# Tile 0's expert dots: from the sweep over all experts to gathered rows

## The chip, the core and the metric

The kernel runs on one core of a Trainium2 chip. The metric is the device time of one launch in microseconds; three runs of the kernel before gave a median of 3764.14 us (3752.35 to 3771.85).

## The reference

One step of a one-layer hybrid decoder: a prompt of 1024 tokens and eight sequences of four sample tokens. Each layer projects the normed input, runs dilated attention and an RWKV-7 scan, projects out, and then applies PEER, a layer of 16,384 single-neuron experts of which each token uses 128 (8 heads of 16). All of the change is in PEER:

```python
def one(hb):                                   # hb: tokens x 1024
    q = (hb @ w_pq).reshape(chunk, PEER_HEADS, 2, PEER_HALF)
    s = jnp.einsum('nhpc,hpkc->nhpk', q, sub_keys).astype(jnp.float32)
    ...                                        # top 16 of 256 sums per head: eid, gate
    act = jax.nn.gelu(jnp.einsum('nd,nhkd->nhk', hb, expert_u[eid]), approximate=False)
    return jnp.einsum('nhk,nhkd->nd', gate * act, expert_v[eid])
```

For one token this is the sum over its 128 experts of gate x gelu(u . h) x v, with u and v rows of 1024 numbers of the tables `expert_u` and `expert_v`.

## The kernel before

The prompt's 1024 tokens are eight tiles of 128; the 32 sample tokens are a ninth, `NT`. PEER is computed in two ways.

- **By gathered rows** (tiles 5, 6, 7 and `NT`, 416 units in all). A unit is one of the 128 picks of each token of a tile. `gathered` lets POOL issue an indirect DMA that fetches 128 rows of 4 KB (one per token) of `expert_u`; VectorE multiplies them by h2 and sums along the row in one instruction (tile `row`, result in a column of `co`). h2 stands in PSUM there (tile `gh`), and so does the running sum of the second half, in which the rows of `expert_v` are gathered, scaled by `co` and added (tiles `gh` and `ga`). Five `row` buffers are in use.
- **Densely** (tiles 0 to 4, 640 tokens). All 16,384 experts are evaluated for all tokens on TensorE, in 128 blocks of 128 experts, and a table of gates that is zero where an expert was not picked selects. `hidden(b)` multiplies the block's `expert_u` by h2T, each operand split into a high and a low part (`uh`, `ul`), so three matmuls for each of 8 pieces of the depth, in two halves of 320 tokens; then gelu on ScalarE, a product with the gates `g` and a split into `ch`, `cl` on ScalarE and VectorE. `output` multiplies these by the block's `expert_v` rows (`vh`, `vl`), in groups of four blocks, for 5 tiles x 2 halves of the columns, and VectorE adds the result to `dacc`. POOL makes `ul` and most of `vl`.

The table of gates, `g_d` in DRAM, is written in the front part by `spread_gates`: for each token TensorE multiplies two one-hot rows (`oha`, scaled by the gate, made by POOL and ScalarE; `ohb`, made by VectorE) into a 128 x 128 table (PSUM tag `sp`), ScalarE copies it to `stage`, and SP stores it.

The program has three parts that matter here. Up to about 700 us come norms, projections and the first scans. In the front part (to 1702 us) several generators are woven: `delta`, the last two RWKV scans, with high priority, and beside it as fill `front` (out-projection and h2 of a tile), `scores`, `picks` (which ends with `eid`, the experts' numbers), `spreads` and `attention`; after `delta` the sample's scan and attention take its place. In the dense part the 128 blocks are fill, and `gather_all` with the routing of tiles 6, 7 and `NT` is the main stream. A scheduler turns the woven program into one fixed order per engine, and each engine runs its order strictly in turn. The metered costs in `_Meter` decide how the generators are woven.

All instructions are issued through one helper, so the profile shows line 196 (197 in the changed kernel) for nearly all; operations are told apart by their tiles.

Of the kernel before, what the change touches and what calls it, by code (L numbers as in the profile page):

```python
# [11 lines left out]
FT = mybir.dt.float32  # L12
FR = mybir.dt.float32r
# [6 lines left out]
D = 1024  # L20
# [19 lines left out]
NROW = 5  # L40
NW = 3
# [160 lines left out]
def tile_hybrid_step(ctx, tc, ins, outs):  # L202
# [1077 lines left out]
    def project_out(pa, pp, tiles, new_x1, new_h2, bufs=NW):  # L1280
# [34 lines left out]
        for j, i in enumerate(tiles):  # L1315
# [28 lines left out]
            if i not in dense_set:  # L1344
# [72 lines left out]
    def route_pick(pick, tops, i, eng=ve):  # L1417
# [5 lines left out]
        fi = pa.tile([128, 16, TOPK], FT, tag="tf", name="tf", bufs=1)[:, :2 * nh]  # L1423
# [29 lines left out]
        pf = pa.tile([128, H, TOPK], I32, tag="te", name="te", bufs=1)[:, :nh]  # L1453
        ve.tensor_scalar(pf, pu.bitcast(I32), 14, None, op0=OP.logical_shift_left)
# [41 lines left out]
    dots = {}  # L1496

# [55 lines left out]
    def spread_gates(pa, pp, i, c0, iota128, stages):  # L1553

        eid, gts = eids[i][i], gates[i][i]
        keys = pa.tile([128, 2, 128], I32, tag="keys", name="keys", bufs=1)
# [58 lines left out]
    def dense(pa, pp, acc, h2T, tiles):  # L1615
# [7 lines left out]
        def hidden(b):  # L1623
# [9 lines left out]
            for h in range(2):  # L1633
                if b % 4 == 0:
                    G_[h] = pa.tile([128, n // 64, 4, 32], FT, tag="g", name="g", bufs=3)
                    sy.dma_start(G_[h], g_d[n // 64 * h:n // 64 * (h + 1), :, b:b + 4].rearrange("s e i t -> e s i t"))
                cs = slice(h * n // 2, (h + 1) * n // 2)
                ps = pp("d")
                for k in range(KD):
                    mm3(ps[:, :n // 2], (uh[:, k], ul[:, k]), [x[:, k, cs] for x in h2T], k == 0, k == KD - 1)  # L1640

                t = ps[:, :n // 2]
                sc.activation(t, t, AF.Gelu)
                tv = t.rearrange("p (s t) -> p s t", t=32)
                ve.tensor_tensor(tv, tv, G_[h][:, :, b % 4], op=OP.mult)
                split(t, ch[:, cs], cl[:, cs])
# [130 lines left out]
    dense_set = [0, 1, 2, 3, 4]  # L1777
# [9 lines left out]
    h2_f = dram.tile([128, KD, NDENSE], FT, name="h2_f")  # L1787
    hcol = {i: 128 * i for i in dense_set}
    with ExitStack() as es:
# [5 lines left out]
        open_picked(es, "picked_A", dense_set, 2)  # L1795
# [204 lines left out]
```

## Time and profile before

| | |
|---|---|
| median of 3 runs | 3764.14 us (3752.35 to 3771.85) |
| the profiled execution's own time | 3753.1 us |
| its span | 3751.3 us |
| mean granted TensorE clock | 0.967 |
| TensorE, VectorE, POOL, ScalarE busy | 92%, 72%, 55%, 38% |
| first dense matmul | 1704 us |

"Busy" of an engine is the time in which one of its instructions runs. Matmuls overlap each other, so their cost is read from start to start, not from their duration. A `DMA_INDIRECT` row of POOL is the issue alone; the data land later. What a stretch costs is read from the windows of that stretch, and what holds an engine up from what it waited for.

### The profile page before, as it was taken

What the parts mean: (1) busy time and instruction counts of PE and PEld (TensorE: products, weight loads), DVE (VectorE), ACT (ScalarE), POOL (GpSimd) and SP (SyncE); (2) the same over time, 40 slices, a digit from 0 to 9 for tenths busy, and PEclk for the clock granted to TensorE, in tenths of its full rate; (3) what the DMA queues carried; (4) which work ended last, traced back from release to release, by engine and by line L of the source; (5) the groups of instructions that cost most, each with busy time, mean ns of one, the idle gap of its engine ahead of it and who ended that gap; (6) DMA issues with size and microseconds to landing.
All of it is one profiled execution on the core that took longest, in us unless ns stands there. A gap on an engine that the chain in (4) does not pass through costs nothing.

```text
span 3751.3 us, 57270 instructions
## 1 busy us (share of the span) xinstructions
PE 3453.9 (92%) x19618; PEld 2873.9 (77%) x19618; DVE 2693.2 (72%) x6059; ACT 1431.2 (38%) x3122; POOL 2080.6 (55%) x1842
## 2 busy tenths in 40 slices
PE   7999999789888988988999989999999999999998
PEld 3878678567767755556777778988888888898997
DVE  2556365588688656785778998787777877777787
ACT  5645345336765754543221122322223222222321
POOL 2342011015545446754655677777777777776784
PEclk8999999899999989998999999999999999999999
DMA  9653596553675568749988779999999999999997
GB/s 293 197 148 117 176 285 186 151 182 130 225 233 166 189 229 255 244 149 309 320 316 298 262 255 334 340 321 322 327 323 324 329 320 322 315 330 318 336 336 256
DMA packets 592528, 981.58 MB, mean 262 GB/s; under 512 B 78323, under 2 KB 354620, under 8 KB 589420
## 3 DMA queue, kind: packets, MB, share of 16 engines
q1 hardware_dynamic: 467788, 524.84, 43.9%
q0 software_dynamic: 124448, 453.08, 34.1%
q8 instruction: 155, 2.54, 0.3%
q14 instruction: 137, 1.12, 0.1%
HBM read 882.97 MB, written 94.78 MB: 261 GB/s over the span
## 4 chain that ended last, share of the span: by engine, by line
PE 51%; DMA 18%; DVE 14%; issue 7%; POOL 6%; ACT 3%; SPq 1%; POOLq 0%; DVEq 0%; ACTq 0%
PE d L196 23%; PE at L196 10%; PE rw L196 5%; PE pj L196 5%; DMA u<-in_uT 5%; PE rs L196 3%; POOL row L196 3%; DMA row<-in_expert_v,eid 3%; PE sp L196 2%; POOL vl L196 2%; DVE gh L196 2%; DVE ohb L196 1%; DMA v<-in_expert_v 1%; DMA w<-wq_d 1%; POOL ul L196 1%
## 5 line engine op out<-in xcount | busy, mean ns | idle before, releaser
L196 PE MATMUL d<-h2T,uh 128*128 128x320 f32 x4096 | 907.3, 311 | 18.1 <-DVE cl L196 9.0
L196 PEld LDWEIGHTS d<-h2T,uh 128*128 128x128 f32 x4096 | 689.6, 189 | 26.6 <-ACT h2T L196 8.2
L196 PE MATMUL d<-h2T,ul 128*128 128x320 f32 x2048 | 633.3, 311 | 0.6 <-POOL ul L196 0.6
L196 PE MATMUL d<-vl,ch 128*128 128x512 f32 x1280 | 508.3, 398 | 42.9 <-POOL vl L196 42.9
L196 DVE CUSTOM_DVE_ANT_0 row<-row,gh 128x1024 f32<-128x1024 f32 x416 | 500.4, 1215 | 63.5 <-DMA row<-in_expert_u,eid 50.7
L196 POOL DMA_INDIRECT row<-in_expert_u,eid x416 | 394.7, 949 | 242.0 <-DVE co L196 89.6
L196 PE MATMUL d<-vh,cl 128*128 128x512 f32 x1280 | 504.5, 395 | 0.0
L196 PE MATMUL d<-vh,ch 128*128 128x512 f32 x1280 | 478.3, 396 | 17.2 <-DVE cl L196 9.7
L196 POOL DMA_INDIRECT row<-in_expert_v,eid x416 | 397.1, 955 | 166.2 <-issue 46.2
L196 POOL TENSOR_SCALAR oha<-c_iota,tr 128x128 f32<-128x128 f32 x320 | 307.4, 966 | 312.1 <-PE sp L196 293.6
L196 POOL TENSOR_TENSOR ul<-u,uh 128x512 fp32r<-128x512 f32 x256 | 332.2, 1306 | 151.7 <-ACT uh L196 143.3
L196 ACT CAST vh<-v 128x512 fp32r<-128x512 f32 x256 | 158.8, 622 | 674.9 <-DMA v<-in_expert_v 451.9
L196 DVE SCALAR_TENSOR_TENSOR gh<-row,co,gh 128x1024 f32<-128x1024 f32 x285 | 366.1, 1285 | 48.6 <-DMA row<-in_expert_v,eid 46.7
L196 PEld LDWEIGHTS d<-h2T,ul 128*128 128x128 f32 x2048 | 386.2, 189 | 5.0 <-issue 3.7
L196 POOL TENSOR_TENSOR wl<-w,wh 128x1024 fp32r<-128x1024 f32 x50 | 123.0, 2461 | 387.2 <-ACT wh L196 326.8
L196 PEld LDWEIGHTS d<-vl,ch 128*128 128x128 f32 x1280 | 244.1, 191 | 108.0 <-POOL vl L196 58.6
L196 POOL TENSOR_TENSOR vl<-v,vh 128x512 fp32r<-128x512 f32 x224 | 289.0, 1301 | 45.7 <-ACT vh L196 42.7
L196 PEld LDWEIGHTS d<-vh,ch 128*128 128x128 f32 x1280 | 242.7, 190 | 77.5 <-DVE dacc L196 12.7
L196 ACT CAST uh<-u 128x512 fp32r<-128x512 f32 x256 | 154.8, 621 | 367.3 <-DMA u<-in_uT 212.2
L196 PEld LDWEIGHTS d<-vh,cl 128*128 128x128 f32 x1280 | 243.9, 191 | 52.8 <-issue 2.5
L196 DVE TENSOR_TENSOR dacc<-dacc,d 128x512 f32<-128x512 f32 x310 | 206.2, 683 | 47.8 <-PE d L196 47.6
L196 DVE TENSOR_TENSOR d<-d,g 128x320 f32<-128x320 f32 x256 | 126.8, 496 | 155.6 <-ACT d L196 142.4
(449 smaller groups left out, 6779.4 us busy)
## 6 DMA issues: line engine op xcount, KB each, us to landing
u<-in_uT SPq DMA_DIRECT2D x256, 256.0 KB
v<-in_expert_v SPq DMA_DIRECT2D x256, 256.0 KB
w<-wq_d SPq DMA_DIRECT2D x224, 256.0 KB
g_d<-stage SPq DMA_DIRECT2D x20, 2048.0 KB
g<-g_d SPq DMA_DIRECT2D x64, 640.0 KB
w<-in_w_in SPq DMA_DIRECT2D x75, 512.0 KB
w<-in_w_out SPq DMA_DIRECT2D x112, 256.0 KB
adaw<-in_ada_w SPq DMA_DIRECT2D x32, 512.0 KB
```

What stands on the lines that cost most here:

```text
L196: return f(*a, **k)
```

## The change

Tile 0 stays in the table and in the product with `expert_v`, but no longer in the product with `expert_u`. Its 128 units are dotted in the front part from gathered rows (`early_dots`, two `row` buffers, h2 as `h2e` in SBUF), gelu is applied, and gate x gelu takes the place of the gate in the table. So `hidden` runs over four tiles, 512 tokens in one go, and copies tile 0's part of the table straight into `ch` and `cl`. `spread_gates` takes signed values for tile 0 (three ScalarE instructions where there were two). The spreads run in the order 1, 2, 3, 0, 4, since tile 0's waits for its dots. To make room, several buffers are shared or fewer: `x1` uses the `h2A` ring, h2 of the next tile waits for the scores of the one before it, and tile 5's attention comes after `delta` instead of beside it.

```diff
@@
+NEARLY = 2
@@ project_out
-            if i not in dense_set:
+            if i not in hidden_set:
@@ after expert_dots
+    def early_dots(gat, i):
+
+        eid, gate = eids[i][i], gates[i][i]
+        h2 = gat.tile([128, D], FT, name="h2e")
+        sy.dma_start(h2, h2_d[i])
+        co = gat.tile([128, 128], FT, name="coe")
+        for j in range(128):
+            t = gat.tile([128, D], FT, tag="row", name="row", bufs=NEARLY)
+            gp.indirect_dma_start(out=t, out_offset=None, in_=A["expert_u"],
+                                  in_offset=bass.IndirectOffsetOnAxis(ap=eid[:, j:j + 1], axis=0))
+            ve.tensor_tensor_reduce(out=t, in0=t, in1=h2, scale=1.0, scalar=0.0, op0=OP.mult, op1=OP.add,
+                                    accum_out=co[:, j:j + 1])
+            yield
+        sc.activation(co, co, AF.Gelu)
+        ve.tensor_tensor(gate, co, gate, op=OP.mult)
+        yield
@@ spread_gates
-                        sc.activation(a[:, j], a[:, j], AF.Relu, scale=ng[:, t], bias=tr[:, 2, t])
+                        if signed:
+                            sc.activation(a[:, j], a[:, j], AF.Relu, scale=-1.0, bias=1.0)
+                            sc.activation(a[:, j], a[:, j], AF.Copy, scale=tr[:, 2, t])
+                        else:
+                            sc.activation(a[:, j], a[:, j], AF.Relu, scale=ng[:, t], bias=tr[:, 2, t])
@@ dense, hidden
-            for h in range(2):
-                if b % 4 == 0:
-                    G_[h] = pa.tile([128, n // 64, 4, 32], FT, tag="g", name="g", bufs=3)
-                    sy.dma_start(G_[h], g_d[n // 64 * h:n // 64 * (h + 1), :, b:b + 4].rearrange("s e i t -> e s i t"))
-                cs = slice(h * n // 2, (h + 1) * n // 2)
-                ps = pp("d")
-                for k in range(KD):
-                    mm3(ps[:, :n // 2], (uh[:, k], ul[:, k]), [x[:, k, cs] for x in h2T], k == 0, k == KD - 1)
-
-                t = ps[:, :n // 2]
-                sc.activation(t, t, AF.Gelu)
-                tv = t.rearrange("p (s t) -> p s t", t=32)
-                ve.tensor_tensor(tv, tv, G_[h][:, :, b % 4], op=OP.mult)
-                split(t, ch[:, cs], cl[:, cs])
+            if b % 4 == 0:
+                G_[0] = pa.tile([128, n // 32, 4, 32], FT, tag="g", name="g", bufs=2)
+                sy.dma_start(G_[0], g_d[:, :, b:b + 4].rearrange("s e i t -> e s i t"))
+            ps = pp("d")
+            for k in range(KD):
+                mm3(ps, (uh[:, k], ul[:, k]), [x[:, k] for x in h2T], k == 0, k == KD - 1)
+
+            sc.activation(ps, ps, AF.Gelu)
+            v = lambda x: x.rearrange("p (s t) -> p s t", t=32)
+            ve.tensor_tensor(v(ps), v(ps), G_[0][:, 4:, b % 4], op=OP.mult)
+            split(ps, ch[:, 128:], cl[:, 128:])
+            split(G_[0][:, :4, b % 4], v(ch)[:, :4], v(cl)[:, :4])
@@ the front part
-    dense_set = [0, 1, 2, 3, 4]
+    dense_set, hidden_set = [0, 1, 2, 3, 4], [1, 2, 3, 4]
+    NHID = 128 * len(hidden_set)
...
-            if len(h2A) < 2 or ("scores", max(h2A) - 1) in ready:
+            if not h2A or ("scores", max(h2A)) in ready:
...
-            for tiles in ([2, 3], [4], [5]):
+            for tiles in ([2, 3], [4]):
...
+        def early():
+            yield from until(0)
+            yield from early_dots(gat0, 0)
+            ready.add("acts")
+
         def spreads():
-            for i in dense_set:
-                yield from until(i)
-                yield from spread_gates(ps_, p_at, i, 128 * i, iota, stages)
+            for i in [1, 2, 3, 0, 4]:
+                yield from until(i if i else "acts")
+                yield from spread_gates(ps_, p_at, i, 128 * i, iota, stages, i not in hidden_set)
...
-        streams = [front(), scores(), picks(), spreads()]
+        streams = [front(), scores(), picks(), spreads(), early()]
...
+                yield from attn_prompt(px, "left", [5])
+                ready.add(("mix", 5))
```

What the fixed order makes of it is shown at two places. The first is POOL in the front part, where the picks of a tile (`tq`) and the spread's one-hots stand. Before, behind the picks of tile 1:

```order
L196 TENSOR_TENSOR tq<-td,te 128x800
L196 TENSOR_SCALAR oha<-c_iota_6639,tr_7962 128x128
L196 TENSOR_TENSOR tq<-td,te 128x800
L196 TENSOR_SCALAR oha<-c_iota_6639,tr_7962 128x128 x37
L196 TENSOR_SCALAR neg<-tr_10099 128x128 x2
L196 TENSOR_SCALAR oha<-c_iota_6639,tr_10099 128x128 x59
```

And now, behind the same picks:

```order
L197 TENSOR_TENSOR tq<-td,tp 128x800
L197 DMA row<-in_expert_u,eid_7522 128x1024 x3
L197 TENSOR_SCALAR neg<-tr_8544 128x128 x2
L197 TENSOR_SCALAR oha<-c_iota_6645,tr_8544 128x128 x2
L197 DMA row<-in_expert_u,eid_7522 128x1024
L197 TENSOR_SCALAR oha<-c_iota_6645,tr_8544 128x128
L197 DMA row<-in_expert_u,eid_7522 128x1024
L197 TENSOR_SCALAR oha<-c_iota_6645,tr_8544 128x128 x2
L197 DMA row<-in_expert_u,eid_7522 128x1024
```

The gathers of tile 0 (`DMA row<-in_expert_u`) stand between the one-hots, one to three apart, and the first spread is tile 1's. The 128 gathers reach up to the end of the second spread; on VectorE 125 of the 128 dots stand ahead of the last state update (`S`) of `delta`.

The second place is VectorE at the program's end: the sums of tile 7's gathered values (`gh`) and the last additions of the dense part (`dacc`). Before:

```order
L196 SCALAR_TENSOR_TENSOR gh<-row,co,gh 128x1024
L196 TENSOR_TENSOR d<-d,g 128x320
L196 SCALAR_TENSOR_TENSOR gh<-row,co,gh 128x1024
L196 TENSOR_TENSOR cl<-d,ch 128x320
L196 TENSOR_TENSOR row<-gh,row 128x1024
L196 TENSOR_TENSOR dacc<-dacc,d 128x512
```

And now:

```order
L197 TENSOR_TENSOR dacc<-dacc,g_31962 128x512
L197 TENSOR_TENSOR fx<-fx,dacc 128x512
L197 SCALAR_TENSOR_TENSOR gh<-row,co,gh 128x1024
L197 TENSOR_TENSOR fx<-fx,dacc 128x512
L197 SCALAR_TENSOR_TENSOR gh<-row,co,gh 128x1024 x2
L197 TENSOR_TENSOR fx<-fx,dacc 128x512
L197 SCALAR_TENSOR_TENSOR gh<-row,co,gh 128x1024 x81
L197 TENSOR_TENSOR row<-gh,row 128x1024
```

Before, the last sum stood ahead of the last dense additions; now 81 sums stand behind everything of the dense part. In between, from the 80th to the 120th block, POOL's order holds 44 gathers in eight blocks where it held 52.

## Rows read from the trace of the kernel before

**Rows 1.** The page: span, busy time by engine, the chain by engine.
```profile
span 3751.3 us, 57270 instructions
...
PE 3453.9 (92%) x19618; PEld 2873.9 (77%) x19618; DVE 2693.2 (72%) x6059; ACT 1431.2 (38%) x3122; POOL 2080.6 (55%) x1842
...
PE 51%; DMA 18%; DVE 14%; issue 7%; POOL 6%; ACT 3%; SPq 1%; POOLq 0%; DVEq 0%; ACTq 0%
```

**Rows 2.** Windows: front beside delta, front after it, dense early, dense late, end.
```profile
core 0: us, PE busy (x) PEld busy (x) DVE busy (x) ACT busy (x) POOL busy (x), PEclk, DMA share, GB/s
840.00:1290.00 450.00, 403.55 (x2550) 340.96 (x2551) 351.75 (x1294) 304.78 (x745) 232.12 (x224) 0.97 0.58 188
1290.00:1702.00 412.00, 346.01 (x1876) 214.99 (x1875) 287.95 (x829) 207.44 (x501) 240.60 (x176) 0.91 0.66 219
1702.00:2300.00 598.00, 566.64 (x2912) 466.73 (x2913) 481.21 (x1110) 153.32 (x299) 384.49 (x352) 0.97 0.87 296
2300.00:3712.00 1412.00, 1367.87 (x7579) 1232.26 (x7578) 1094.05 (x1567) 390.52 (x785) 1051.17 (x976) 0.99 0.94 327
3712.00:3752.00 40.00, 27.93 (x125) 22.89 (x124) 26.05 (x36) 2.72 (x5) 4.29 (x3) 0.88 0.46 156
```

**Rows 3.** Windows: where VectorE, and where the DMA engines, are busiest.
```profile
2100.00:2200.00 100.00, 81.64 (x446) 74.11 (x445) 95.85 (x272) 28.57 (x55) 71.08 (x62) 0.95 0.78 247
2300.00:2400.00 100.00, 99.24 (x554) 89.95 (x553) 77.74 (x94) 29.25 (x59) 74.40 (x69) 1.00 0.98 343
```

**Rows 4.** Timeline of PE, hidden matmuls: start us, us, operation.
```profile
2299.61 0.31 PE L196 MATMUL d<-h2T,ul 128*128 128x320 f32 x1
2299.76 0.46 PE L196 MATMUL d<-h2T,uh 128*128 128x320 f32 x2
2300.05 0.31 PE L196 MATMUL d<-h2T,ul 128*128 128x320 f32 x1
```

**Rows 5.** Timeline of PE, output matmuls, first and last of 13.
```profile
2322.05 0.39 PE L196 MATMUL d<-vh,ch 128*128 128x512 f32 x1
...
2324.78 0.39 PE L196 MATMUL d<-vh,ch 128*128 128x512 f32 x1
```

**Rows 6.** Groups from 2300 to 3712 us: busy us, mean ns, idle before.
```profile
L196 PE MATMUL d<-h2T,uh 128*128 128x320 f32 x3130 | 687.6, 309 | 0.0
...
L196 POOL DMA_INDIRECT row<-in_expert_v,eid x324 | 309.0, 954 | 109.2 <-issue 39.8 <-DVE gh L196 27.5 <-DVE co L196 18.8
...
L196 POOL DMA_INDIRECT row<-in_expert_u,eid x288 | 273.5, 950 | 127.1 <-DVE co L196 38.8 <-issue 34.5 <-DVE ga L196 32.7
```

**Rows 7.** Page, DMA issues: count, KB each, us to landing.
```profile
u<-in_uT SPq DMA_DIRECT2D x256, 256.0 KB
v<-in_expert_v SPq DMA_DIRECT2D x256, 256.0 KB
...
g<-g_d SPq DMA_DIRECT2D x64, 640.0 KB
```

**Rows 8.** Tiles eid (800 to 900 us) and S: duration min/median/max, first and last start.
```profile
L196 DVE TENSOR_REDUCE eid<-tq x8: 964/994/1009, 833.4 to 849.5; 128x16 int32<-128x800 uint32 x8
...
L196 DVE SCALAR_TENSOR_TENSOR S<-rw,PC,c_mask_bd x32: 296/344/356, 856.4 to 1281.2; 128x128 f32<-128x128 f32 x32
```

**Rows 9.** Tile gh: dots of tiles 6 and 7; last sums.
```profile
L196 DVE CUSTOM_DVE_ANT_0 row<-row,gh x256: 1203/1217/1225, 2553.4 to 3424.6; 128x1024 f32<-128x1024 f32 x128
...
L196 DVE SCALAR_TENSOR_TENSOR gh<-row,co,gh x127: 1274/1286/1293, 3431.9 to 3716.0; 128x1024 f32<-128x1024 f32 x127
```

**Rows 10.** Tiles ohb, oha (840 to 1702 us) and vl (2300 to 3712 us).
```profile
L196 DVE TENSOR_TENSOR ohb<-c_iota,tr x320: 372/424/4642, 855.0 to 1669.2; 128x256 f32<-128x256 f32 x160
...
L196 POOL TENSOR_SCALAR oha<-c_iota,tr x320: 781/894/3439, 855.1 to 1665.8; 128x128 f32<-128x128 f32 x160
...
L196 DVE TENSOR_TENSOR vl<-v,vh x24: 690/1232/3427, 2341.4 to 3643.8; 128x512 fp32r<-128x512 f32 x24
```

**Rows 11.** Page, DMA issues: gathered rows, median us from issue to landing.
```profile
row<-in_expert_u,eid POOLq DMA_INDIRECT x416, 6.2
```

More of the change, by code (lines that the diff above doesn't have):

```diff
@@ L1422, in route_pick @@
         eid, gate = (x[i][i][:, :TOPK * nh] for x in (eids, gates))
-        fi = pa.tile([128, 16, TOPK], FT, tag="tf", name="tf", bufs=1)[:, :2 * nh]
+        fi = iu.bitcast(FT)
         ve.tensor_copy(fi, iu)
@@ L1452, in route_pick @@
         yield
-        pf = pa.tile([128, H, TOPK], I32, tag="te", name="te", bufs=1)[:, :nh]
-        ve.tensor_scalar(pf, pu.bitcast(I32), 14, None, op0=OP.logical_shift_left)
+        pf = pu.bitcast(I32)
+        ve.tensor_scalar(pf, pf, 14, None, op0=OP.logical_shift_left)
         sh = [128, TOPK, NCAND]
@@ L1551, in tile_hybrid_step, with spread_gates @@
     g_d = dram.tile([NDENSE // 32, 128, 128, 32], FT, name="g_d")
-    def spread_gates(pa, pp, i, c0, iota128, stages):
+    def spread_gates(pa, pp, i, c0, iota128, stages, signed=False):
         eid, gts = eids[i][i], gates[i][i]
-        keys = pa.tile([128, 2, 128], I32, tag="keys", name="keys", bufs=1)
+        keys = pa.tile([128, 2, 128], FT, tag="ohb", name="keys", bufs=3).bitcast(I32)
         ve.tensor_scalar(keys[:, 0], eid, 7, None, op0=OP.arith_shift_right)
@@ L1786, in tile_hybrid_step @@
     open_picked(ctx, "picked_5", [5])
-    h2_f = dram.tile([128, KD, NDENSE], FT, name="h2_f")
-    hcol = {i: 128 * i for i in dense_set}
+    h2_f = dram.tile([128, KD, NHID], FT, name="h2_f")
+    hcol = {i: 128 * j for j, i in enumerate(hidden_set)}
     with ExitStack() as es:
@@ L1794, in tile_hybrid_step @@
         pp = open_psum(ed, "deltap", rw=2, py=1)
-        open_picked(es, "picked_A", dense_set, 2)
+        open_picked(es, "picked_0", [0])
+        open_picked(es, "picked_A", hidden_set, 2)
+        gat0 = open_pool(es, "gat0")
         ps_ = open_pool(es, "spread")
@@ L1820, in new_x1 @@
         def new_x1(i):
-            return pf.tile([128, D], FT, tag="x1", name="x1", bufs=1)
+            return pf.tile([128, D], FT, tag="h2A", name="x1", bufs=2)
         def front():
@@ L1873, in tile_hybrid_step @@
             pc = open_pool(e2, "atts", "right")
-            rest = weave(*((g, c) for g, c in zip(streams, (True, True, False, False))), (last(), True))
+            rest = weave(*((g, c) for g, c in zip(streams, (True, True, False, False, False))), (last(), True))
             run(weave((rwkv_sample(lambda tag: other("rs"), "right"), True), (attn_sample(lambda tag: other("rs"), "right", pc), True), fill=[rest]))
@@ L1878, in tile_hybrid_step @@
     hpd = open_pool(ctx, "h2T", "right")
-    h2T = [hpd.tile([128, KD, NDENSE], FR, name=f"h2T{s}") for s in range(2)]
+    h2T = [hpd.tile([128, KD, NHID], FR, name=f"h2T{s}") for s in range(2)]
     pa = open_pool(ctx, "dense")
     acc = pa.tile([128, len(dense_set), 2, 512], FT, name="dacc")
-    hf = acc.rearrange("p a b c -> p (a b c)").rearrange("p (k t) -> p k t", k=KD)
+    hf = acc[:, :len(hidden_set)].rearrange("p a b c -> p (a b c)").rearrange("p (k t) -> p k t", k=KD)
     with tc.high_priority(offset=AHEAD):
```

## The prediction

> **What bounds the kernel now.** The page comes first: PE is busy 92% of the span, VectorE 72%, POOL 55%, and half of the chain that ended last lies on PE [rows 1]. An average over stages with different limits decides nothing, so the windows come next [rows 2]. Beside `delta` (840 to 1290 us) PE is busy 404 of 450 us and VectorE 352; so PE leads, with VectorE 78% full. In the late dense part (2300 to 3712 us) PE is busy 1368 of 1412 us while the DMA engines are 94% busy at 327 GB/s, and the most that they show in any 100 us is 98% at 343 GB/s [rows 2, 3]. Two limits lie close together there. The rows of operations then give the size of the unit that the change cuts.
>
> **Dense part, what goes.** Three hidden matmuls of 320 columns take 0.44 us from start to start (2299.61 to 2300.05), 0.147 each [rows 4]. A block has 2 halves x 8 pieces x 3 = 48 of them: 7.04 us. The output's matmuls of 512 columns take 2.73 us for twelve steps, 0.2275 each [rows 5]; a block has 10 products of 3, so 6.83 us. PE's work per block is 13.87 us. In the window 3130 matmuls with `uh` ran, 32 per block, so 97.8 blocks in 1412 us: 14.44 us per block [rows 2, 6].
> After the change a block has 24 hidden matmuls of 512 columns. Priced like the output's, they take 5.46 us, so PE's work is 12.29 us, 1.58 less.
> The transfers do not shrink with it: u and v are 4 x 256 KB per block and g half of a 640 KB load [rows 7], in all 1.38 MB. A gather moves 128 x 4 KB = 0.524 MB. The order puts 44 gathers beside eight blocks where it had 52, so 5.5 per block: 4.26 MB. At the 343 GB/s of the best window that is 12.4 us, at the window's mean of 327 it is 13.0. PE needs 12.29. Now the block takes 4% more than PE's work alone; with PE and the transfers equally long I take 12.9 us, within 12.4 to 13.0. Over 97.8 blocks that is -151 us (-200 to -141).
> The first 30.2 blocks lie in 1702 to 2300 us. PE has 30.2 x 1.58 = 48 us less to do, but it was already idle 31 us there, and from 2100 VectorE is 96% busy [rows 2, 3]. I take -38 us (-48 to -20).
> The epilogue (gelu, gates, split) goes from two passes of 320 columns to one of 512, and of tile 0's 128 columns only the split is left. It lies beside the next block's matmuls and counts as nothing. Uncovered, a pass in one piece would hold up the output at most once per group of four blocks.
>
> **Dense part, what comes back.** With fewer gathers beside each block, the rest is left over: 81 sums of tile 7 now stand behind the last dense addition on VectorE. Before, the last sum started at 3716.0, with the end of the dense part [rows 9]. In that tail PE has nothing to do. A sum takes 1.286 us on VectorE, so no less than 104 us; POOL issues in 0.95 us each [rows 6], so it isn't POOL; 0.524 MB at 343 GB/s is 1.53 us, so the transfer leads: 124 us. The upper end has an issue of 0.95, a landing of 6.2 [rows 11] and the sum one behind the other, 8.4 us over five buffers, 1.69 each: 137. The dense part is therefore shorter by 38 + 151 - 124 = 65 us, not by the 202 us that 128 x 1.58 would give.
>
> **Front part, what is added.** 128 gathers and 128 dots. The picks of tile 0 end at 849.5 + 1 us, the last state update of `delta` starts at 1281.2 [rows 8], and the order puts 125 of the dots between these two on VectorE. A dot of 128 x 1024 takes 1.22 us where its second operand is in PSUM [rows 9]: 128 x 1.22 = 156 us, onto an engine that has 98 us free in this window. VectorE becomes the bound: 352 + 156 = 508 us of work against 450.
> The new dot reads both operands from SBUF, and no row before shows that shape beside POOL. The nearest are `ohb`, also from SBUF alone, at least 372, median 424, at most 4642 ns while POOL runs its own operations, and VectorE's `vl`, at least 690, median 1232 ns; the dots with an operand in PSUM stay within 1203 to 1225 [rows 9, 10]. So an instruction that reads SBUF twice waits for POOL's, and the other way round `oha` on POOL ranges from 781 to 3439 ns. The extra per dot lies between 0 and 0.54 us (the median of `vl` above its least); I take 0.4, as POOL will be over half busy with one-hots and gathers: 50 us.
> The Trainium skill, SBUF — State Buffer (SBUF: two separate sides), has the rule: VectorE and GpSimd share one pair of ports as an exclusive lock, which VectorE takes in two-port modes and for two SBUF inputs, and while a two-port instruction holds it GpSimd can't write the descriptors of its DMAs. The rows on `ohb` and `vl` agree as to computing; no run here shows it for descriptors. By the rule in full the front would grow as in the second rival below, by the rows as in the next paragraph.
> VectorE's work beside `delta` is then 558 us. The most that it is busy in any 100 us is 96% [rows 3]; at 95% the window lasts 587 us, +137. The ends: without extra and at 100%, 508, +58; with 0.54 each and at today's share of 78%, 738, +288.
> The wait for landing costs little by itself: with two buffers, a pair takes 6.2 + 1.2 us [rows 9, 11], so 128 rows need 64 x 7.4 = 474 us, less than the window. The gathers queue on POOL among the one-hots, so behind a gather that waits for a buffer stand one-hots that PE waits for; that cost is in the 95%.
> PE's work in the front is the same apart from 8 transposes. ScalarE gets 64 instructions more for the signed table, some 0.4 us each, in 1290 to 1702 us, where it is busy 207 of 412 us. Tile 5's attention moves into that window, and scores of a tile move out of it, since a fixed share of PE's work stands ahead of `delta`'s end in both orders. I take +4 us (-20 to +20). The shared `h2A` ring makes h2 of a tile wait for the scores before it; it lies beside VectorE's excess and counts as nothing.
>
> **Sum.** +137 + 4 - 65 = +76 us on the profiled execution's 3753.1 us: 3829. That execution is 11 us below the median of the runs, 3764, within their spread; I give 3830.
>
> **Rivals.**
> - *The front swallows the dots, and the kernel is faster.* VectorE has 98 us free beside `delta` and 124 in 1290 to 1702 us [rows 2], 222 together, more than the dots' 156, and PE, not VectorE, led both windows. If `delta` has the first right on VectorE and what is late moves into the second window, the front grows by little, say 10 us: 3753 + 10 - 65 = 3698. Against it: the order puts the dots ahead of `delta`'s end, and an engine keeps its order. It is faster than before from a growth under 65 us on.
> - *VectorE and POOL lock each other out.* Each dot waits for a whole one-hot (median 0.89 us [rows 10]) and each gather for a dot. VectorE: 352 + 156 + 114 = 622, at 95% 655, +205; with 4 and -65: 3897. For it: the long tails of `ohb` and `oha` [rows 10]. Against it: their medians lie near their least.
> - *The transfers bound the dense part.* If a block falls only to 13.6 us, the 94% of 14.44 in which the DMA engines were busy, the gain is 82 instead of 151: 3753 + 141 - 38 - 82 + 124 = 3898. Against it: fewer gathers per block.
>
> **Chances.** About 0.5% (19 us) is what a measurement of this kernel can tell from no change. The forecast 0.56; the front swallows 0.18; lock-out 0.16; transfers 0.10. From the first rival 0.15 is faster by more than that and 0.03 the same; of the forecast 0.08 falls within 19 us, where the front grows by some 65 us, its low end, and 0.01 below. Faster 0.16, same 0.11, slower 0.73. The range runs from 3715, a growth of the front by 27 us and so into the first rival, to 3915, above the times of the two others; 0.12 lies below and 0.07 above.
>
> **What would show it.** Right: VectorE over 90% busy from the first dot to the end of `delta`, and the first dense matmul near 1845 instead of 1704; hidden matmuls of 512 columns at 0.23 us; a block near 12.9 us; about 124 us at the end with PE idle and only `gh` and gathers. The dots' mean near 1.6 us shows the lock, 1.2 would refute it. Wrong: a first dense matmul under 1765, or a block over 13.4 us.

## The result and the profile after

The changed kernel takes 4024.69 us (median of four runs, 4018.93 to 4039.63) against 3762.36 us for the kernel before (four runs): 1.071 times as long, 95% interval 1.068 to 1.074. Its profiled execution has a span of 4022.7 us, 271 more than before. The direction was forecast, the size was not: 4025 lies 195 us above the forecast and outside the range. By stages, read from the first matmul on `h2T` of each block and the last one (all us):

| term | before | after | measured change | forecast |
|---|---|---|---|---|
| first dense matmul at | 1704 | 1923 | +219 | +141 |
| blocks 0 to 32, per block | 19.03 | 17.69 | -43 | -38 (30.2 blocks) |
| blocks 32 to 128, per block | 14.58 | 14.11 | -45 | -151 (97.8 blocks) |
| last hidden matmul to the end | 39 | 179 | +140 | +124 |
| span | 3751 | 4023 | +271 | +76 |

The page's first lines and the chain's shares, as [rows 1] had them:

```profile
span 4022.7 us, 51646 instructions
...
PE 3379.0 (84%) x16554; PEld 2598.1 (65%) x16554; DVE 2892.3 (72%) x6188; ACT 1398.2 (35%) x3059; POOL 2260.8 (56%) x1970
...
PE 15%; DMA 14%; DVE 8%; issue 5%; POOL 5%; ACT 1%; POOLq 0%; DVEq 0%; SPq 0%; ACTq 0%
PE d L197 13%; DMA u<-in_uT 9%; DMA row<-in_expert_v,eid 3%; POOL row L197 3%; DVE gh L197 3%; PE at L197 2%; DMA row<-in_expert_u,eid 2%; POOL vl L197 1%; DVE row L197 1%; DVE cl L197 1%; DMA v<-in_expert_v 1%; DVE dacc L197 1%; POOL ul L197 1%; DVE ga L197 0%; DVE d L197 0%
```

No engine's share of the span grew by more than a point (POOL from 55% to 56%); PE fell from 92% to 84%, and the loads of u make 9% of the span on the chain, where they made 5%. Time went into waits. The windows, which answer to [rows 2], are now beside `delta`, the rest of the front, the dense part early and late, and the tail:

```profile
core 0: us, PE busy (x) PEld busy (x) DVE busy (x) ACT busy (x) POOL busy (x), PEclk, DMA share, GB/s
840.00:1475.00 635.00, 460.88 (x2483) 369.07 (x2481) 500.87 (x1675) 279.05 (x680) 370.24 (x321) 0.87 0.71 231
1475.00:1903.00 428.00, 356.84 (x1965) 225.31 (x1966) 287.25 (x718) 246.82 (x643) 278.10 (x209) 0.91 0.68 225
1903.00:2500.00 597.00, 546.79 (x2273) 405.36 (x2272) 484.43 (x1078) 150.46 (x280) 382.55 (x347) 0.96 0.86 293
2500.00:3877.00 1377.00, 1273.66 (x5263) 1007.78 (x5261) 1043.14 (x1406) 353.66 (x677) 976.28 (x894) 0.96 0.89 304
3877.00:4022.00 145.00, 0.00 (x0) 0.00 (x0) 115.40 (x93) 0.00 (x0) 75.12 (x80) 0.50 0.90 320
```

Beside `delta` VectorE has 501 us of work, as forecast without a lock (508), but in 635 us: 79% busy, where over 90% was to show that it bounds. The last state update (`S`) of `delta` starts at 1470 us, where it started at 1281. In the late dense part PE's share fell from 97% to 92% and the DMA share from 0.94 to 0.89, so neither has become the limit. The tail is 145 us with no PE at all.

The tiles of the front (duration min/median/max in ns, first and last start in us). A tile's "pick" here is the moment when its `eid` is complete; `keys<-eid` hands it to the tile's spread (here tiles 1 and 2); `ohb` is VectorE's part of the spreads:

```profile
L197 DVE CUSTOM_DVE_ANT_0 row<-row,h2e x128: 1194/1224/2495, 826.6 to 1462.8; 128x1024 f32<-128x1024 f32 x128
...
L197 DVE SCALAR_TENSOR_TENSOR S<-rw,PC,c_mask_bd x32: 326/341/347, 864.6 to 1470.2; 128x128 f32<-128x128 f32 x32
...
L197 DVE TENSOR_SCALAR keys<-eid x2: 215/217/219, 943.4 to 943.5; 128x128 int32<-128x128 int32 x2
...
L197 DVE TENSOR_SCALAR keys<-eid x2: 219/220/221, 1225.6 to 1225.8; 128x128 int32<-128x128 int32 x2
...
L197 DVE TENSOR_TENSOR ohb<-c_iota,tr x320: 393/420/4782, 952.5 to 1872.4; 128x256 f32<-128x256 f32 x160
```

The dots' median, 1224 ns, is that of the dots before with an operand in PSUM, 1217 [rows 9]: no lock of 0.4 us. The spreads run to 1872 where they ran to 1669 [rows 10]. They are not the last thing in the front. TensorE's own rows there (start us, us, operation, and in brackets the idle time before it and what ended it) are the last matmuls of the spreads (`sp`), of the attention (`at` from `pT`), of the out-projection behind it (`at` from `m`), and the first dense one:

```profile
1877.48 0.38 PE L197 MATMUL sp<-oha,ohb 128*128 128x128 f32 x2
...
1890.09 2.47 PE L197 MATMUL at<-pT,vr 128*64 128x128 f32 x32
...
1918.86 4.76 PE L197 MATMUL at<-w,m 128*128 128x256 f32 x14 [14.24 <-DMA m<-mix_d]
1923.27 0.82 PE L197 MATMUL d<-h2T,uh 128*128 128x512 f32 x2
```

So two paths end close together: the spreads at 1878 us, and at 1893 the attention that follows `delta`. In the kernel before they ended at 1670 and 1689.

### The profile page after: what moved, and what is told of

Read it like the earlier page. It is cut to its first block, busy times and chain, and to the rows that moved or that the text cites. A ratio compares the mean times of both kernels' runs of the same rounds, so it can differ in the third digit from the quotient of the medians.

```text
span 4022.7 us, 51646 instructions
## 1 busy us (share of the span) xinstructions
PE 3379.0 (84%) x16554; PEld 2598.1 (65%) x16554; DVE 2892.3 (72%) x6188; ACT 1398.2 (35%) x3059; POOL 2260.8 (56%) x1970
## 5 line engine op out<-in xcount | busy, mean ns | idle before, releaser
L197 POOL DMA_INDIRECT row<-in_expert_u,eid x544 | 530.2, 975 | 426.9 <-DVE coe L197 81.3
L197 PE MATMUL d<-h2T,uh 128*128 128x512 f32 x2048 | 644.9, 396 | 0.4 <-ACT uh L197 0.4
L197 PE MATMUL d<-vh,ch 128*128 128x512 f32 x1280 | 500.2, 413 | 77.7 <-DVE dacc L197 41.2
L197 PE MATMUL d<-vl,ch 128*128 128x512 f32 x1280 | 521.3, 408 | 49.2 <-POOL vl L197 49.1
L197 PEld LDWEIGHTS d<-h2T,uh 128*128 128x128 f32 x2048 | 384.3, 188 | 98.4 <-issue 3.3
L197 POOL TENSOR_SCALAR oha<-c_iota,tr 128x128 f32<-128x128 f32 x320 | 346.3, 1088 | 160.0 <-PE sp L197 146.6
L197 PE MATMUL d<-h2T,ul 128*128 128x512 f32 x1024 | 407.8, 398 | 0.6 <-POOL ul L197 0.6
L197 PE MATMUL sp<-oha,ohb 128*128 128x128 f32 x1280 | 222.9, 312 | 93.9 <-DVE ohb L197 35.0
L197 PEld LDWEIGHTS sp<-oha,ohb 128*128 128x128 f32 x1280 | 194.5, 216 | 146.9 <-issue 66.5
L197 PE MATMUL at<-w,h2A 128*128 128x256 f32 x768 | 215.3, 414 | 54.7 <-DMA w<-wq_d 38.9
```

Source lines behind the costliest of these rows:

```text
L197: return f(*a, **k)
```

## Experiments

A stretch, a block or a first matmul is meant as in the table above; "changed" is the changed kernel. Its two disputed parts are the front (+219 instead of +141) and the late block (14.11 instead of 12.9). Six executions whose front has the changed kernel's order on TensorE (the changed kernel, e4, e5, e9, e10 and e18) put the first dense matmul at 1919 to 1937 us and tile 2's pick at 1218 to 1235, so differences under some 20 us say nothing there. Most runs were executed once.

**The front: which of dots, gathers and order.** Edit of e1 (the spreads wait for the pick of tile 0 alone):

```diff
-            yield from early_dots(gat0, 0)
```

> Leaves out tile 0's 128 gathers and dots (the table holds its bare gates); all else is as in the changed kernel. There delta's last S update is at 1470 us, the first dense matmul at 1923; before the change 1281 and 1704. Theory: the gathers and dots are the whole of the front's growth: S near 1281 to 1300, first dense matmul 1700 to 1740. Rival: the rearrangement (spread order, shared h2A ring, tile 5's attention moved) costs a good part: first dense matmul 1780 or later. The dense part should be as in the changed kernel, 14.1 us per block from the 32nd block on.

Measured: 3903.2 us, first dense matmul 1836, last state update 1232: `delta` is back, and the front is still 132 us longer than before. The rival was right: most of the loss isn't from the added work. Tiles `keys` (tiles 1 and 2) and `ohb` of e1:

```profile
L197 DVE TENSOR_SCALAR keys<-eid x2: 220/220/220, 916.3 to 916.4; 128x128 int32<-128x128 int32 x2
...
L197 DVE TENSOR_SCALAR keys<-eid x2: 217/219/221, 1135.4 to 1135.5; 128x128 int32<-128x128 int32 x2
...
L197 DVE TENSOR_TENSOR ohb<-c_iota,tr x320: 361/424/4206, 920.4 to 1784.5; 128x256 f32<-128x256 f32 x160
```

The spreads are one chain of five tiles, some 120 to 200 us each, and no tile starts before its pick is there. Before, tile 0 ran 855 to 1000 and tile 1 1007 to 1142, so tile 2 could start at 1155, when its pick had come: the chain never stood still for over 20 us. With the order 1, 2, 3, 0, 4 it starts at 920 (65 us later), is through tile 1 at 1056, and stands until 1142 for tile 2's pick (86 us). In the changed kernel the same pause goes from 1108 to 1234. Two runs put the order to the test by itself (in e6 tile 0's numbers and gates also get buffers of their own, since they are needed longer):

```diff
 e6, kernel before:   -            for i in dense_set:
                      +            for i in [1, 2, 3, 0, 4]:
 e7, e1 and:          -            for i in [1, 2, 3, 0, 4]:
                      +            for i in [0, 1, 2, 3, 4]:
```

> The kernel before, with one part of the change alone: the spreads run in the order 1, 2, 3, 0, 4 (tile 0's numbers and gates get their own buffers, so that they live long enough). Theory: the spreads are a chain of their own, about 160 us each, that ends just before the dense part; starting with tile 1 it begins some 70 to 100 us later and stands still again until tile 2 is picked: last one-hot 80 to 150 us later than 1669 us, total 3830 to 3900. Rival (the other rearrangements or VectorE's load set the front): total 3750 to 3790.

> The changed kernel without tile 0's gathers and dots (the table holds its bare gates) and with the spreads in the order 0 to 4. Theory (order of the spreads): the first dense matmul, at 1836 us without dots in the order 1, 2, 3, 0, 4, comes back to 1690 to 1730. Rival (shared h2A ring, tile 5's attention later): it stays above 1790.

e6 took 3896.4 us against 3770.3 for the kernel before on the same chip, first dense matmul 1861 instead of 1704. e7 took 3809.2, first dense matmul 1705 instead of 1836, with all the other rearrangements of the change in place: these cost nothing that shows at the front's end. The order alone costs 131 to 157 us of the first dense matmul. In e7 that is less than the spreads gain: they end at 1563 instead of 1805, and the attention, which ends at 1669, then sets the rest. The rows of e6 (`keys` of tile 1, then of tiles 2 and 3):

```profile
L196 DVE TENSOR_SCALAR keys<-eid x2: 217/218/220, 915.6 to 915.7; 128x128 int32<-128x128 int32 x2
...
L196 DVE TENSOR_SCALAR keys<-eid x4: 207/216/314, 1138.2 to 1185.8; 128x128 int32<-128x128 int32 x4
...
L196 DVE TENSOR_TENSOR ohb<-c_iota,tr x320: 373/424/4391, 923.6 to 1823.4; 128x256 f32<-128x256 f32 x160
```

**The front: the other 87 us (1836 to 1923).** e2 keeps the dots on a tile that no gather fills, e3 the gathers, of which VectorE reads one column:

```diff
 e2  -            gp.indirect_dma_start(out=t, ...)
     -            ve.tensor_tensor_reduce(out=t, in0=t, in1=h2, ...)
     +            ve.tensor_tensor_reduce(out=t, in0=h2, in1=h2, ...)
 e3  -            ve.tensor_tensor_reduce(out=t, in0=t, in1=h2, ...)
     +            ve.tensor_copy(co[:, j:j + 1], t[:, :1])
```

> Keeps the 128 dots (on h2e itself) and leaves out the gathers of tile 0, so no dot waits for a row. Theory that the wait for landing with two row buffers is a good part of the growth (VectorE stood 96 us before dots): last S update at 1370 to 1400 us instead of 1470, VectorE over 88% busy from 840 us to it. Rival that VectorE's added work alone sets it: 1440 or later.

> Keeps the 128 gathers and lets VectorE read one column of each row in place of the dot, so the wait for landing stays and the 160 us of dots go. Theory of the wait: last S update at 1360 to 1400 us, still 80 us or more above 1281. Rival, VectorE's work: below 1330.

e2: 3988.9 us, first dense matmul 1883, last state update 1455, which is the rival's side (1440 or later). Its dots no longer depend on the pick and ran from 731 to 992 us, partly ahead of tile 0's pick, which came at 902 instead of 839 in the changed kernel. e3: 3995.1 us, first dense matmul 1931, last state update 1334, between its theory (1360 to 1400) and its rival (below 1330), with VectorE 64% busy up to it.

The two runs are long by different paths. In e2 the spreads end at 1802 and the attention behind `delta` at 1856; in e3 the spreads end at 1897 and the attention at 1774. So the dots alone make the front 47 us longer than e1's, through `delta`, and the gathers alone 95 us, through the spreads. In the changed kernel both paths are late, and taking the load off one alone gains little: without the dots' work (e3) the front ends no earlier, without the gathers (e2) 40 us earlier. Three runs took the gathers apart, all with VectorE reading two of the 128 rows only (e13 without `h2e`, which makes room):

```diff
 e11, e13, e17  +            if j % 64 == 63:
                +                ve.tensor_copy(co[:, j - 63:j + 1], t[:, :64])
 e13            -NEARLY = 2
                +NEARLY = 3
 e17            -            t = gat.tile([128, D], FT, tag="row", ...)
                +            t = gat.tile([128, 128], FT, tag="row", ...)
                             ... in_=A["expert_u"].rearrange("e (a c) -> (e a) c", a=8) ...
```

> The changed kernel with all 128 gathers of tile 0's rows in the front part, but VectorE reads only every 64th of the rows that land (the dots are left out, so tile 0's activations are not the reference's). The gathers then wait for landings only at their buffers, and VectorE waits only twice. Theory 'VectorE stands in its order behind rows that have not landed': the first dense matmul comes from 1923 (with dots) and 1931 (gathers with a one-column read each) down to 1836 to 1860, as in the run without gathers and dots. Rival 'POOL and the transfers': the 128 issues of 1 us on POOL and the landings hold up the picks and the spread whether VectorE reads or not: 1900 to 1935.

> As the run with gathers whose rows VectorE does not read (two of 128 read, tile 0's dots left out), but with three row buffers instead of two. Theory 'POOL stands in its order at gathers whose buffer has not landed, and the picks and one-hots queued behind it come late': POOL's 124 us of waits for landings in 840 to 1240 us fall by at least a half, tile 2's pick ends at 1135 to 1175 instead of 1203 (1133 without gathers), and the first dense matmul comes at 1840 to 1885 instead of 1911. Rival 'POOL's 1 us per issue and the transfers': pick of tile 2 at 1190 to 1215 and the first dense matmul at 1895 to 1925, as with two buffers.

> As the run whose gathered rows VectorE does not read (two buffers; tile 0's dots left out), but each of the 128 gathers fetches 512 bytes per index instead of 4 KB (8 MB in all instead of 64 MB; the data are of other rows). Theory 'bytes': the transfers of the front part that PE waits for are no longer slowed: DMA share of 840 to 1200 us near 0.6 instead of 0.85, tile 2's pick ends at 1135 to 1170 us, first dense matmul at 1840 to 1875. Rival 'POOL's issues of 1 us ahead of the picks and one-hots': pick at 1185 to 1215, first dense matmul at 1890 to 1925 as with whole rows.

| run | tile 2's pick | first dense matmul |
|---|---|---|
| e1, no gathers | 1135 | 1836 |
| e17, 512 bytes per index | 1198 | 1891 |
| e11, whole rows, unread | 1204 | 1911 |
| e13, whole rows, unread, three buffers | 1219 | 1929 |
| e3, one column read | 1196 | 1931 |
| changed, dots | 1226 | 1923 |

In all the runs of this table but the last the attention is through 120 us or more before the spreads, so the spreads' path is the late one. e11 refuted VectorE's waits for landings as the cause of the late spreads. e13 was to refute POOL's waits for its buffers, but took only a fifth of them away (98 of 124 us are left from 840 to 1240 us); e17 halves them (60 us) and moves an eighth of the bytes, and the pick comes 6 us earlier than in e11. So neither these waits nor the bytes make up most of it. The windows from 840 to 1200 us of e1, e11 and e17, columns as above:

```profile
840.00:1200.00 360.00, 323.47 (x1919) 265.20 (x1919) 274.51 (x1105) 198.05 (x484) 126.02 (x117) 0.94 0.56 172
```

```profile
840.00:1200.00 360.00, 286.38 (x1602) 227.01 (x1603) 230.52 (x860) 162.74 (x393) 195.18 (x186) 0.91 0.85 282
```

```profile
840.00:1200.00 360.00, 274.04 (x1497) 219.61 (x1496) 231.20 (x893) 156.06 (x378) 219.65 (x213) 0.87 0.56 171
```

With an eighth of the bytes the DMA share is back at 0.56, yet PE still gets less done than without gathers and the pick stays late. What e17 has in common with the others is 128 issues of 1 us on POOL, which also computes parts of the picks (`tq`) and of the one-hots (`oha`) and takes them in order: POOL's busy time goes from 126 to 220 us. By the numbers the rival of e17 holds, and that of e13 but for 4 us (its pick and its first dense matmul came 4 us above the rival's ranges). One thing stays open: leaving work out also changes how the other streams are woven, so the fixed order of the other instructions differs from run to run of this table. e2, without a gather, has its pick of tile 2 at 1227 too, after a late start: from tile 1's pick to tile 2's it takes 219 us in e1 and in e2, and 251 to 282 in the five runs with gathers. No run holds the weave with everything but the issues as it was, so that POOL's issues are the cause is argued, and how the 87 us divide between issues and weave isn't settled.

**The late block: the table ahead of u.** One load of the table goes out for every four blocks. First the loads were left out but for the first, in the changed kernel (e4) and in the one before (e8):

```diff
-            if b % 4 == 0:
+            if b == 0:
```

> Loads the table of gates for the first group of four blocks only and uses it for all (31 loads of 1280 KB left out). In the changed kernel u is issued behind the table's load once per group and lands 16 us later, and a block takes 13.93 us from the 80th to the 112th. Theory (u waits behind the table): 12.6 to 13.1 us per block, PE idle under 0.6 us per block where it was 1.0. Rival (the gathers' fixed order on VectorE and POOL holds PE up): 13.6 or more.

> The kernel before with the table loaded for the first group of four blocks only. There PE has 13.87 us of work in a block of 14.58. Theory (the matmuls that the change removes had covered u's wait behind the table): little to gain, 14.0 to 14.3 us per block, 30 to 60 us in all. Rival (the load costs the same 1.3 us per block in both kernels): under 13.9 isn't possible by PE's work, so 13.9, 65 us or more in all, and the change would have lost nothing by it.

e4: 3799.0 us, block 12.79. e8: 3702.5 us, block 14.04. The loads cost a block of the changed kernel 1.32 us and one of the kernel before 0.54. Without them the block is what was forecast (12.9). (e4's total is lower still because its order leaves 52 sums behind the last hidden matmul where the changed kernel leaves 97.) The chain of the changed kernel shows how, once per group (start us, us, what):

```profile
3404.03 1.33 POOL ul L197 x2
3405.35 16.05 DMA u<-in_uT
```

SP's queue in the same place (start us, us, operation) has the 1280 KB of the table issued right ahead of that u:

```profile
3402.49 0.38 SPq L197 DMA_DIRECT2D g<-g_d  x1
3405.35 18.45 SPq L197 DMA_DIRECT2D u<-in_uT  x4
```

and the waits from 2500 to 3900 us (total us, times, longest) hand it on: u to ScalarE's rounding, that to POOL's `ul`, and POOL, in its order, to the `vl` that PE needs:

```profile
ACT uh L197 <- DMA u<-in_uT: 231.2, 54, 13.3
POOL ul L197 <- ACT uh L197: 176.7, 24, 10.2
...
PE d L197 <- POOL vl L197: 44.5, 29, 4.1
```

Four runs ask what about the load it is: e5 and e10 put it earlier in the program on SP's queue, e9 on ScalarE's queue, e18 with the table laid out so that a partition reads one run of 10 KB instead of 20 pieces of 512 bytes (its store and its load follow the new layout):

```diff
 e5   +            if grp < ngrp - 1:
      +                table(grp + 1)            # after values(grp, 0)
 e10  +                    if (dh, tt) == (0, 1):
      +                        table(grp + 2)    # amid the output of grp
 e9   -                sy.dma_start(G_[0], g_d[...])
      +                sc.dma_start(G_[0], g_d[...])
 e18  -    g_d = dram.tile([NDENSE // 32, 128, 128, 32], FT, name="g_d")
      +    g_d = dram.tile([32, 128, NDENSE // 32, 4, 32], FT, name="g_d")
```

> The changed kernel, all bytes kept, with the load of a group's table issued amid the output of the group before instead of among the u loads of its own. Without 31 of 32 table loads a block took 12.79 us instead of 14.11. Theory: the place in the queue is what costs (u waits some 16 us behind 1280 KB): 12.9 to 13.3 us per block from the 32nd on. Rival: the bytes themselves cost: 13.8 or more.

> The changed kernel with the table of a group of four blocks loaded a whole group earlier on SP's queue (amid the output of the group before the one before), so that it is never the load that VectorE waits for; the same bytes, still with u loads right behind it in the queue. Theory 'place in the queue': the u behind it is late as before, block 13.9 to 14.2. Rival 'the table itself is what comes late': block under 13.4.

> The changed kernel with one word changed: the table of four blocks is loaded through ScalarE's queue, so that the u halves that are issued behind it on SP's queue no longer stand behind its 1280 KB; bytes and piece sizes are as they were. Theory 'place in the queue': u lands in time, a block of blocks 32 to 128 falls from 14.11 us to 12.8 to 13.3, PE's idle time there from 96 us to under 40, the span by 80 to 130 us. Rival 'bytes': the 16 DMA engines have too much to carry while the table comes, whichever queue it is on, and u comes late all the same: block 13.8 to 14.2, span within 30 us of 4023.

> The changed kernel with the table laid out in memory so that a group's load is one run of 10 KB per partition instead of 20 pieces of 512 bytes; still on SP's queue ahead of u, still 1280 KB, and the front part's writes are 512-byte pieces. Theory 'time that the load holds the queue': the 1280 KB pass faster and u comes sooner: block 13.0 to 13.6 instead of 14.11, PE idle 20 to 60 us. Rival 'only the place counts': 13.9 to 14.2. Rival 'pieces alone cure it, as in the kernel before': 12.8 to 13.0. The writes cost the front part 15 to 35 us as they did in the kernel before (27).

e5: 4016.9 us, block 14.11. e10: 4016.6, block 13.90. Neither moved the load: with two buffers SP can't issue it before the table of two groups earlier has been read for the last time, and in all three kernels it goes out 0.03 us after that (median of 20 groups), right ahead of u loads. In e10 that is 65 us before the table is first used, in the changed kernel 66 (medians too). One such pair in the changed kernel, the load and its first use:

```profile
2658.32 0.38 SPq L197 DMA_DIRECT2D g<-g_d  x1
...
2734.38 0.70 DVE L197 TENSOR_TENSOR d<-d,g 128x512 f32<-128x512 f32 x1 [11.62 <-ACT d L197]
```

So e5 and e10 decide nothing, but these rows do: the table itself is not what comes late. e9: 3886.0, block 12.84, and e18: 3902.4, block 12.79, each as good as no loads at all. e9 and e18 from 2500 to 3650 us:

```profile
2500.00:3650.00 1150.00, 1126.19 (x4832) 907.79 (x4831) 942.17 (x1298) 335.28 (x637) 896.96 (x823) 0.99 0.95 333
```

```profile
2500.00:3650.00 1150.00, 1130.00 (x4863) 912.32 (x4862) 944.51 (x1299) 334.62 (x630) 901.42 (x826) 1.00 0.94 337
```

The same bytes now pass at 333 and 337 GB/s, where the changed kernel moved 304, and the block is 1.3 us shorter: so the transfers' total wasn't the bound. It is the load in 512-byte pieces that holds SP's queue in front of u, and either cure will do (e18 was expected at 13.0 to 13.6; its rival, that larger pieces alone cure it, was right). SP's waits from 2500 to 3650 us, in the changed kernel and in e18, say that it isn't SP's wait for the table's buffer (`DVE d`), which is no shorter in e18; what shrinks is its wait for loads of u to land:

```profile
SPq L197 <- DMA u<-in_uT: 161.9, 22, 10.8
...
SPq L197 <- DVE d L197: 24.8, 12, 4.5
```

```profile
SPq L197 <- DMA u<-in_uT: 75.4, 27, 5.6
SPq L197 <- DVE d L197: 38.1, 17, 4.5
```

**The same in the kernel before, and a version faster than both.** e12 takes ScalarE's queue there, e14 puts the load of half a table two blocks ahead in the program, e15 does that with the layout of e18 (runs of 5 KB; store and load follow it):

```diff
 e12       -                    sy.dma_start(G_[h], g_d[...])
           +                    sc.dma_start(G_[h], g_d[...])
 e14, e15  +                if b % 4 == 2 and h == 0 and b < 124:
           +                    half(b // 4 + 1, 0)
 e15       +    g_d = dram.tile([32, 128, NDENSE // 32, 4, 32], FT, name="g_d")
```

> The kernel before with the two 640 KB halves of the table loaded through ScalarE's queue instead of SP's, nothing else. Theory 'place in the queue': the u halves no longer stand behind the table; the part of a block that the table costs there (14.58 us with, 14.04 without the loads) mostly goes: block 14.05 to 14.25, total 3700 to 3730 us, 0.98 to 0.99 of the kernel before. Rival 'bytes': 3755 to 3775, no change. If ScalarE is held up at the load by a buffer that is not free yet, it is slower: above 3785.

> The kernel before with the first half of a group's table (640 KB) loaded two blocks before the group, in the third buffer that stands ready for it, and the second half at the group's start as before: on SP's queue u then stands behind 640 KB twice per group instead of behind 1280 KB once. Theory 'one lump in front of u': the block falls from 14.58 us toward the 14.04 without loads, 14.1 to 14.4, total 3705 to 3745 us, ratio 0.985 to 0.996. Rival 'bytes': no change, 3750 to 3770.

> As the run before it, and the table in memory laid out so that a half of a group's table is one run of 5 KB per partition instead of 512-byte pieces (the writes of the front part are then 512-byte pieces, 42 MB of them). Theory 'one lump': 0 to 15 us less than with the half loaded ahead alone, since large pieces take some 20 to 25 per cent less of the DMA engines' time per byte; the writes cost the front part 0 to 10 us. Rival 'pieces decide': 25 us or more below that run.

e12: ratio 1.002 [1.000, 1.004], no change; e14: 1.001 [0.999, 1.003], no change; both are where their rivals ("bytes") had them. e15: 3713.5 us against 3756.7, ratio 0.988 [0.984, 0.992]: faster than both kernels. In e12 the wait moved to VectorE (2300 to 3650 us):

```profile
DVE d L196 <- DMA g<-g_d: 100.1, 19, 9.6
```

So the table itself now comes late. ScalarE doesn't issue it late: the second half of a group's table goes out 0.04 us after its buffer is free and 15.6 us before its first use (medians of 20 groups; 0.03 and 13.0 on SP's queue in the kernel before). With three half buffers that is all the lead there is, where the changed kernel's two whole buffers gave 66 us; that a fourth half buffer would make e12 pay is argued and wasn't tried. e14 changed nothing in what ran: in the kernel before, too, the first half goes out 64 us before its use, 3.9 us behind the second half of the group before it. So what e15 adds in effect is the layout, and it comes out 49 us below e14 where its rival, "pieces decide", had 25 or more. e15 from 2300 to 3650 us:

```profile
2300.00:3650.00 1350.00, 1345.12 (x7533) 1223.21 (x7533) 1092.51 (x1564) 387.41 (x777) 1053.32 (x978) 1.00 0.95 341
```

PE is 99.6% busy, block 13.93, against PE's own 13.87. Of the gain of 62 us over 96 blocks 27 are lost in the front, whose first dense matmul moved to 1731 (1704 to 1712 in three executions with the same order on TensorE and the old layout), more than the 0 to 10 that was expected of writing in 512-byte pieces; that the writing costs it is argued. In e18, which writes so too, the first dense matmul came at 1937, within the changed kernel's scatter.

**The tail.** e16 is e9 with `NROW = 6` for `NROW = 5`, a row buffer more for the gathered sums.

> The changed kernel with its table on ScalarE's queue and six row buffers for the gathered sums instead of five, which in the order moves 43 of the 81 sums that stood behind the last hidden matmul ahead of it. Theory of the tail as forecast (about 1.5 to 1.75 us a sum with the PE idle): the time from the last hidden matmul to the end falls from 187 to 105 to 125 us, while a block costs 0.2 to 0.5 us more as the sums go into it (12.84 to 13.0 to 13.4): span 3835 to 3875 against 3884. Rival 'the tail only moves': span within 10 us of 3884.

Measured: 3886.3 us, span 3884.5 against 3884.2. From the last hidden matmul to the end, e9 and e16:

```profile
3698.00:3884.00 186.00, 26.57 (x114) 20.79 (x112) 154.77 (x137) 2.76 (x5) 97.56 (x102) 0.58 0.90 319
```

```profile
3776.00:3884.00 108.00, 26.61 (x116) 21.32 (x114) 96.62 (x91) 3.03 (x5) 57.34 (x57) 0.64 0.88 328
```

Behind the last hidden matmul 56 sums stand instead of 103, and the end is 78 us shorter: 1.7 us a sum, as expected. But a block went from 12.84 to 13.48 (+61 over 96 blocks, above the expected range), and the first dense matmul came at 1946, 28 us after e9's, with the same order on TensorE: no row explains it, and most of it is within the scatter of 1919 to 1937. By the span the rival was right. Sums put back among the blocks cost there some three quarters of what they cost behind them.

## Why the prediction was wrong

- **"At 95% the window lasts 587 us": failed.** The direction was right: the dots do lengthen `delta` (e2 against e1: last state update 1455 against 1232). But VectorE's 501 us of work filled 79% of the window, not 95%, and its end came 189 us later where 137 was forecast. 78%, the share before, was the low end of the prediction's own range; why it stays there is open, since e2, whose dots wait for no landing, has 81%. By e2 this path alone, `delta` and then the attention, puts the first dense matmul at 1883.
- **"+4" for the rest of the front: failed, by a chain that was put at nothing.** The prediction counted PE's work and passed over the order of the tiles. Taking tile 0 out of the chain's head leaves the spreads waiting for tile 2's pick: 131 to 157 us (e6, e7). The gathers delay that pick by another 60 us or more, 90 in the changed kernel (1135 to 1226), with the last four spreads as long as in e1 (638 and 642 us). This path alone puts the first dense matmul at 1891 to 1931, with no dots' work at all (e3, e11, e13, e17). So +219 came from two paths of nearly equal length, where +141 stood for one of them; the nearness of the two is an accident of this kernel.
- **The extra 0.4 us per dot: refuted.** Mean of a dot 1.265 us, least 1.194. POOL's issues, from 840 to 1240 us, took 1005 ns in e11, with VectorE's dots left out, and 1016 with them. The Trainium skill, SBUF — State Buffer (SBUF: two separate sides), has a VectorE instruction with two SBUF inputs contend with GpSimd's reads of SBUF and keeps the stop of descriptor writing for two-port modes. The trace agrees as to the issues; of the contention with reads it shows little, a mean 0.04 us above the median.
- **"The wait for landing costs little by itself": half right.** VectorE waited more than was reckoned, and `delta` with it (last state update 1334 in e3, which keeps these waits, 1274 in e11, which doesn't); but e11 still ends the front at 1911. The waits in the changed kernel from 820 to 1475 us:

```profile
DVE row L197 <- DMA row<-in_expert_u,eid: 95.7, 52, 6.1
POOL row L197 <- DVE coe L197: 81.3, 33, 8.8
```

- **PE's work per block: right.** Five hidden matmuls of 512 columns take 1.16 us here, 0.23 each:

```profile
2999.63 0.62 PE L197 MATMUL d<-h2T,uh 128*128 128x512 f32 x2
...
3000.79 0.40 PE L197 MATMUL d<-h2T,ul 128*128 128x512 f32 x1
```

- **Block 12.9: failed, by a wait that lost its cover, and with 106 us the largest miss (the front's is 78).** The step "the transfers do not shrink" asked only how many bytes pass, not what stands in front of what. u came late before too, but PE's 13.87 us of work left 0.7 us of it to be seen; at 12.29 it is 1.8. Without the queueing the block is 12.79 to 12.84, inside the forecast's 12.4 to 13.0. The mean granted clock of the late dense part moves with PE's idle time: 0.96 of 2.4 GHz in the changed kernel, where PE is 92% busy, 0.99 and 1.00 in e9 and e18, where it is 98%.
- **First blocks -38 and tail +124: right** in mechanism and nearly in size (-43 and +140). The 81 sums behind the last dense addition take 126 us, from 3891 to 4016, 1.55 each where 1.53 was taken; the other 14 us lie between the last hidden matmul and that addition, where 16 more sums stand.
- **Rivals.** "The front swallows the dots" was right that VectorE has time to spare (79% and 67% busy in the two windows) and wrong about the front. "Transfers bound the dense part" came nearer in its block (13.6) for a reason that e9 and e18 refute. "Lock each other out" fell with the dots' mean.

## What to carry to other kernels

Before a change takes a link out of a serial chain, or puts it elsewhere, follow that chain from its first input to what waits for its end, and look for a second path that ends near it; busy shares show neither. When work that covers a late load is removed, ask what else stands in that load's queue, and try another queue or larger pieces first: here one word was worth 3.4% of the changed kernel (3886 against 4025). Before reading a run that moves a load in the program, look when the load goes out: a buffer that isn't free yet keeps it where it was (e5, e10, e14). Work left over behind the last stage has a price, but moving it back among the stages saves only what is idle there.

## What was not expected of the hardware

At the same DMA share, 0.94 and 0.95, the engines moved 326 GB/s in the kernel before (2300 to 3650 us) and 341 in e15, whose table comes in pieces of 5 KB instead of 512 bytes. A u of 256 KB issued behind the 1280 KB in 512-byte pieces landed 16.05 us later. With 128 gathers in the front tile 2's pick came 60 us later or more, whether they moved 64 MB or 8 MB. On ScalarE's queue the same table load, issued with no less lead, kept VectorE waiting 100 us in all (e12) where on SP's queue, ahead of u, it cost VectorE 5.
